# Fewer products in each step of a blocked recurrence, and a quarter of a gate's matrix product on the vector engine

## The chip, the cores and the metric

The kernel runs on one core of one Trainium2 chip. A core has TensorE (PE, the matmuls; PEld in a profile is its weight loads), VectorE (DVE), ScalarE (ACT), GpSimd (POOL), the queue of SyncE (SP) and 16 DMA engines. The metric is the time of one execution in device microseconds; a figure for a kernel is the median of its runs.

## The reference

One layer of a hybrid block over 256 context and 256 latent tokens with 2048 channels: modulation of a normalised input by SiLU(c), one wide input projection, three mixers (neighbourhood attention, pooling, a two-way recurrence), their merge by sigmoid gates, an output projection, and a gated residual. The two parts that the change touches:

```python
# modulation: shift, scale (used at once) and gate (used at the very end)
m = silu(c) @ w_mod + b_mod                   # (2048,) @ (2048, 6144)
shift, scale, gate = split(m, 3)
...
# mixer C, per head: state S is 64 x 64, [value, key]; 16 heads, 2 directions, 512 tokens
def step(S, inp):
    rt, vt, wt, kt, at, bt = inp
    sa = S @ at
    S = S * wt[None, :] + outer(sa, bt) + outer(vt, kt)
    return S, S @ rt
...
out = merged @ w_out
x_out = rms_norm(x + gate * out, final_g)     # latent tokens only
```

## The kernel before

**Numbers.** Matrix products in full precision are made of three products of rounded pairs: each weight tile is split into a high part (`whi`, ScalarE, line 576) and a low part (`wlo`, VectorE, line 577), and activations into `hh` and `hl`. A product of a tile is then hh x whi, hl x whi and hh x wlo.

**Stage one** (about the first 146 us) runs over 16 slices j of the model dimension. Each pass multiplies `cs`, which holds SiLU(c) of latent and context tokens in its columns 1 and 0, with the slice's modulation weights (`adaln_a`: two loads `wm_0` and `wm_1` of 1 MB, 16 matmul records each into `psm`), turns the sums by two transposes, forms shift and scale (`adaln_b`, `md` on VectorE), writes the normalised input `hh[j]` (ScalarE) and `hl[j]` (VectorE) in `htile`, and adds the slice's part of the first seven column tiles (`first_tiles`, `acc`, 21 matmuls of 512 columns on `shi`, `slo`). `psm` is a single buffer: the products of the next slice can start when VectorE has read the sums of this one. The order on TensorE in this stage is set by the framework's scheduler from its own cost estimates, except for instructions marked `keep_in_program_order`.

**Mixers and merge** (to about 1465 us). TensorE's order is written out by a planner, `Order`. It fills TensorE's time with units, halves of 512 KB weight loads: column tiles of the input projection (`d`, line 871), groups of merge logits and then 12 branch groups (`dg`, lines 582 to 584, the branch groups read `bh` and `bl`). Between units it puts bursts of small streams: attention (`side`), the recurrence of one head pair after the other (`rwkv(p)`, p = 0 to 7), folding of the gate (`gate_out`). A stream yields `(TensorE time, latency)` after each burst and comes up again when the latency has passed in planned time; it yields a name to wait for a mark. Weights come into three `raw` buffers over SP's queue in the same order.

**The recurrence** is worked in chunks of 64 tokens, four of context (q = 0) and four of latent tokens (q = 1), for two heads (par) and two directions (d) at once. `features` and `scores` make, for each chunk, EO (operands with the state, rows of value terms), AT (0:4 the strictly triangular matrix A of the chunk, 4:8 the readout's scores), BKT (B and K turned) and SV (state and values above each other). `inverse` inverts I - A: the diagonal 32 x 32 blocks on VectorE over a trip through DRAM (`dA`, `iA`, `dT`, `AT`), and `merge` the block off the diagonal by two small products (`mp`, 64 records each). `chain` then does eight steps, each of three dependent bursts:

```python
px = EO . SV                    # what the state and the values put in      (line 374)
xs = copy(px);  pu = inverse . xs;  SV <- copy(pu)          # lines 376 to 390
pS = BKT . SV;  SV of the next step <- pS * G + sg          # line 398 to 407
```

and for q = 1 also the readout, `py`, from EO and SV (line 382) and from AT and SV (line 411). `sg` is the old state times the decay, four instructions on GpSimd (line 370). `rwkv(p + 1)` is added to the planner when the merge of pair p is done. After the chain comes `readout`; the last pair's result goes through DRAM into `bh[11]`, `bl[11]`, and the four branch groups of this mixer wait for the mark `rw7`.

**The gate.** `gate_units` loads the gate's 16 MB of modulation weights in 64 pieces of 256 KB (`wg`) between units once the attention is done, and multiplies them with `cs` in 32 bursts of 4 matmuls (`mg`, line 1138). For each quarter cc of the columns, the sums are copied to `gs`, the bias row is loaded into one row of `gs`, and a product with `selg` adds them up over partitions and spreads the sum (`pg`, line 1115), which goes to DRAM (`gd[cc]`) for the output stage.

## Time and profile before

| | us |
|---|---|
| median of 3 runs | 1567.87 (1566.26 to 1570.13) |
| profiled execution | 1565.28 |
| its span on the core | 1563.6 |
| stage one, to the last acc matmul | about 146 |
| branch groups | about 1262 to 1466 |

In a row of the timeline stand the start and the length of an instruction or of a run of equal ones, the engine, the line and the tiles as out<-in with the number of records; in brackets the idle time of the engine before it and what ended it. A matmul of 4-byte numbers that is not split leaves two records. Lengths of matmuls overlap, so the distance of two starts tells what one costs. In a row of groups follow the busy time, the mean length in ns and the idle time before. A row of windows has for each engine the busy time and the number of instructions in the order PE, PEld, DVE, ACT, POOL, then the granted clock of TensorE, the DMA share and GB/s.

### The profile page before, as it was taken

The numbers are of one execution on the slowest core, as the hardware profiler recorded it, in microseconds if no ns is written. First come the engines' busy times: TensorE is split into PE (matmuls) and PEld (weight loads), VectorE is DVE, ScalarE is ACT, GpSimd is POOL, SyncE is SP. The second block draws the span as 40 slices with busy tenths as digits, with TensorE's granted clock in tenths as the row PEclk, the third lists the DMA queues.
The fourth block names the chain that finished last, engine by engine and source line by source line (L and its number), as shares of the span: only waits on it lengthen the run. The fifth ranks groups of instructions, "written<-read, shape, count | busy, mean of one in ns | idle before, by whom it ended". The sixth has DMA issues, their size and how long they took to land.

```text
span 1563.6 us, 32275 instructions
## 1 busy us (share of the span) xinstructions
PE 1510.7 (97%) x12256; PEld 1199.3 (77%) x12256; DVE 1133.1 (72%) x2602; ACT 798.5 (51%) x1599; POOL 248.5 (16%) x438
## 2 busy tenths in 40 slices
PE   7999999999999999999999999999999999998998
PEld 5667878798877897788789877877896665667787
DVE  5345788788887877886887768778777775566664
ACT  4224663575465546544664556356646633334453
POOL 2332010150022022201230230023023200210000
PEclk9999999999999999999999999999999999999999
DMA  9996445545532464243355524523566698878863
GB/s 391 348 330 223 144 143 169 163 152 179 173 126 91 137 180 147 95 132 122 100 175 159 179 77 132 175 104 118 167 198 211 202 299 274 268 242 262 267 207 111
DMA packets 217811, 288.21 MB, mean 184 GB/s; under 512 B 62516, under 2 KB 176308, under 8 KB 213048
## 3 DMA queue, kind: packets, MB, share of 16 engines
q1 hardware_dynamic: 210160, 275.66, 54.3%
q10 hardware_dynamic: 7496, 10.50, 1.9%
q8 instruction: 96, 1.57, 0.4%
q14 instruction: 59, 0.48, 0.1%
HBM read 264.34 MB, written 21.50 MB: 183 GB/s over the span
## 4 chain that ended last, share of the span: by engine, by line
PE 86%; DVE 5%; DMA 4%; ACT 2%; issue 2%; SPq 0%; ACTq 0%; POOL 0%; DVEq 0%; POOLq 0%
PE d L871 36%; PE dg L582 9%; PE dg L583 7%; PE dg L584 7%; PE acc L793 2%; PE o L582 2%; DMA raw<-in_w_br 2%; PE o L584 2%; PE o L583 2%; PE px L374 2%; PE acc L799 1%; PE acc L796 1%; PE pu L388 1%; PE pS L398 1%; PE psm L693 1%
## 5 line engine op out<-in xcount | busy, mean ns | idle before, releaser
L576 ACT CAST whi<-raw 128x512 fp32r<-128x512 f32 x584 | 354.0, 619 | 388.7 <-PE d L871 169.5
L577 DVE TENSOR_TENSOR wlo<-raw,whi 128x512 fp32r<-128x512 f32 x584 | 400.4, 698 | 131.3 <-ACT whi L576 100.0
L871 PE MATMUL d<-hh,whi 128*128 128x256 f32 (+1 forms) x1184 | 367.5, 330 | 1.1 <-ACT mth L967 1.1
L871 PE MATMUL d<-hl,whi 128*128 128x256 f32 (+1 forms) x1184 | 359.3, 323 | 0.0
L871 PEld LDWEIGHTS d<-hh,whi 128*128 128x128 f32 x1184 | 225.4, 190 | 24.3 <-issue 2.9
L871 PE MATMUL d<-hh,wlo 128*128 128x256 f32 (+1 forms) x1184 | 241.4, 323 | 0.0
L871 PEld LDWEIGHTS d<-hl,whi 128*128 128x128 f32 x1184 | 225.9, 191 | 16.2 <-issue 0.2
L871 PEld LDWEIGHTS d<-hh,wlo 128*128 128x128 f32 x1184 | 183.0, 191 | 16.9 <-issue 0.7
L370 POOL TENSOR_SCALAR sg<-SV,G 64x64 f32<-64x64 f32 x192 | 111.4, 586 | 355.7 <-DVE SV L407 194.1
L582 PE MATMUL dg<-whi,hh 128*128 128x512 f32 x384 | 164.0, 427 | 0.4 <-DVE gnag L911 0.3
L584 PE MATMUL dg<-wlo,hh 128*128 128x512 f32 x384 | 150.7, 392 | 0.8 <-DVE wlo L577 0.6
L583 PE MATMUL dg<-whi,hl 128*128 128x512 f32 x384 | 150.6, 392 | 0.0
L582 PE MATMUL dg<-whi,bh 128*128 128x512 f32 x192 | 83.3, 434 | 10.4 <-ACT whi L576 3.0
L582 PEld LDWEIGHTS dg<-whi,hh 128*128 128x128 f32 x384 | 72.0, 187 | 23.6 <-issue 5.9
L584 PEld LDWEIGHTS dg<-wlo,hh 128*128 128x128 f32 x384 | 72.1, 188 | 17.9 <-DVE wlo L577 1.6
L583 PEld LDWEIGHTS dg<-whi,hl 128*128 128x128 f32 x384 | 72.4, 188 | 10.0 <-issue 0.2
L584 PE MATMUL dg<-wlo,bh 128*128 128x512 f32 x192 | 77.5, 404 | 0.5 <-DVE wlo L577 0.5
L583 PE MATMUL dg<-whi,bl 128*128 128x512 f32 x192 | 77.3, 403 | 0.5 <-DMA bl<-bs 0.5
L309 DVE TENSOR_TENSOR iM<-iA,iT 128x126 f32<-128x126 f32 (+22 forms) x248 | 63.6, 257 | 17.3 <-DMA iA<-dA 10.7
L311 DVE TENSOR_TENSOR iT<-iT,iM 128x126 f32<-128x126 f32 (+22 forms) x248 | 62.8, 253 | 6.6
L806 ACT ACTIVATE hh<-xT,md 128x256 fp32r<-128x256 f32 x32 | 17.5, 593 | 90.5 <-DVE md L717 90.5
L1283 DVE TENSOR_TENSOR wl<-raw,wh 128x512 fp32r<-128x512 f32 x64 | 41.3, 686 | 25.2 <-ACT wh L1282 25.0
(329 smaller groups left out, 2488.6 us busy)
## 6 DMA issues: line engine op xcount, KB each, us to landing
raw<-in_w_in SPq DMA_DIRECT2D x244, 512.0 KB, 3.6
wm<-in_w_ms SPq DMA_DIRECT2D x32, 1024.0 KB, 7.0
raw<-in_w_br SPq DMA_DIRECT2D x48, 512.0 KB, 5.5
wg<-in_w_mg SPq DMA_DIRECT2D x64, 256.0 KB, 4.2
raw<-in_w_out SPq DMA_DIRECT2D x32, 512.0 KB, 4.5
wst<-in_w_st SPq DMA_DIRECT2D x16, 448.0 KB, 7.9
sl<-in_bias SPq DMA_DIRECT2D x32, 128.0 KB, 3.0
iA<-dA SPq DMA_DIRECT2D x16, 256.0 KB, 5.4
```

Of the source, the lines that this page charges most:

```text
L309: nc.vector.tensor_tensor(m, A[:, st:st + 1, st + 1:32].to_broadcast([128, ni, nt]), T[:, 0:ni, st:st + 1].to_broadcast([128, ni, nt]), AL ...
L311: nc.vector.tensor_tensor(T[:, 0:ni, st + 1:32], T[:, 0:ni, st + 1:32], m, ALU.add)
L370: nc.gpsimd.tensor_scalar(sg[hv[par], d], SV[hv[par], par, w, d], G[hv[par], gs[d][0], d:d + 1], None, ALU.mult)
L374: nc.tensor.matmul(px[hv[par], d], EO[:, par, d, cs[d], :], SV[:, par, w, d], start=True, stop=True, tile_position=(0, 64 * par))
L576: nc.scalar.copy(hi, src)
L577: nc.vector.tensor_tensor(lo, src, hi.bitcast(F32), ALU.subtract)
L582: nc.tensor.matmul(acc, a[0], b[0], start=start, stop=False)
L583: nc.tensor.matmul(acc, a[1], b[0], start=False, stop=False)
L584: nc.tensor.matmul(acc, a[0], b[1], start=False, stop=stop)
L793: mm = nc.tensor.matmul(acc[i], shi[:, c], hh[j], start=(j == 0), stop=False)
L871: nc.tensor.matmul(box[0], w[m >= 8][:, 128 * i:128 * i + 128], x, start=(v == 0 and m == 0), stop=(v == 3 and m == 11))
L1283: nc.vector.tensor_tensor(l, r, h.bitcast(F32), ALU.subtract)
```

## The change

1. `merge` forms the whole 64 x 64 inverse `An` (a second small product gives its other block) and multiplies it into B (`pw`, for both q) once per pair, and into the readout's scores (`pz`, in step 0). A step then has two bursts: SV takes px directly, and `xs` and `pu` are gone.
2. `sg` is made by two instructions on GpSimd in place of four.
3. `rwkv(p + 1)` is added before the merge of pair p; its first features wait for the mark `merge{p}` where they take the merge's buffers.
4. The first quarter of the gate is made in stage one: 8 loads of 512 KB (`g0w`), 16 multiply-adds on VectorE into `g0`, and one product with ones (`gate_first`). `gate_units` keeps three quarters.
5. `gate_out` comes up 6.5 us of planned time after the last `mg` burst in place of 4.0. The subtraction that writes `hl` is kept in program order.

```diff
 def features(...):
         yield 1.0, 2.2
+        if q == 0 and p:
+            yield f"merge{p - 1}"
...
-    def merge(s, p, psp, ptag):
+    def merge(s, p, psp, ptag, psc, ctag):
-        DN = s.fp.tile([128, 16, 32], F32, tag="up", name=f"DN{p}")
-        P = s.fp.tile([128, 16, 32], F32, tag="E", name=f"mP{p}")
+        An = s.fp.tile([128, 16, 64], F32, tag="E", name=f"An{p}")
+        P = s.fp.tile([128, 16, 32], F32, tag="up", name=f"mP{p}")
         for q in range(2):
-            for r1, r2 in rr:
-                nc.vector.transpose(DN[r1, 8 * q:8 * q + 8], at[q][r1, :, 0:32])
+            nc.vector.transpose(An[:, 8 * q:8 * q + 8], at[q])
+        for r1, r2 in rr:
+            nc.gpsimd.memset(An[r1, :, 32:64], 0.0)
...
-                nc.tensor.matmul(ps2[r1, i], P[r2, i], at[i // 8][r2, i % 8, 32:64], start=True, stop=True,
-                                 tile_position=(64 * h + 32, 64 * h))
+                d2 = at[i // 8][r2, i % 8, 32:64]
+                nc.tensor.matmul(ps2[r2, i], d2, P[r2, i], start=True, stop=True, tile_position=(64 * h + 32, 64 * h + 32))
+                nc.tensor.matmul(ps2[r1, i], P[r2, i], d2, start=True, stop=True, tile_position=(64 * h + 32, 64 * h))
+        for h, (r1, r2) in enumerate(rr):
+            (nc.scalar.copy if h else nc.vector.tensor_copy)(An[r2, :, 0:32], ps2[r2])
...
-        yield 0.9, 2.2
+        yield 1.4, 2.4
+        for q in range(2):
+            pw = (psp, psc)[q].tile([128, 2, 4, 64], F32, tag=(ptag, ctag)[q], name=f"pw{p}_{q}")
+            for d in range(2):
+                for c in range(4):
+                    for par in range(2):
+                        nc.tensor.matmul(pw[hv[par], d, c], An[hv[par], 8 * q + 2 * c + d], s.BKT[p, q][hv[par], par, d, c],
+                                         start=True, stop=True)
+            for par in range(2):
+                (nc.scalar.copy if par else nc.vector.tensor_copy)(s.BKT[p, q][hv[par], par], pw[hv[par]])
+        s.An = An
+        yield 1.8, 2.4
 def chain(...):
-                    for d in range(2):
-                        nc.gpsimd.tensor_scalar(sg[hv[par], d], SV[hv[par], par, w, d], G[hv[par], gs[d][0], d:d + 1], None, ALU.mult)
+                    nc.gpsimd.tensor_tensor(sg[hv[par]], SV[hv[par], par, w], g2[hv[par]].unsqueeze(2).to_broadcast([64, 2, 64]), ALU.mult)
...
-            xs = s.fp.tile([128, 2, 64], F32, tag="xs", bufs=2, name=f"xs{p}_{i}")
-            nc.vector.tensor_copy(xs, px)
...
-            yield (0.9 if q else 0.45), (1.0 if q else 1.6)
-            pu = psp.tile([128, 2, 64], F32, tag=ptag, name=f"pu{p}_{i}")
-            for d in range(2):
-                for par in range(2):
-                    nc.tensor.matmul(pu[hv[par], d], AT[hv[par], cs[d], d, :], xs[hv[par], d], start=True, stop=True)
             for par in range(2):
-                (nc.scalar.copy if par else nc.vector.tensor_copy)(SV[hv[par], par, w], pu[hv[par]])
-            yield 0.4, 2.0
+                (nc.scalar.copy if par else nc.vector.tensor_copy)(SV[hv[par], par, w], px[hv[par]])
+            if i == 0:
+                pz = psy.tile([128, 8, 64], F32, tag=ytag, name=f"pz{p}")
+                at = s.AT[p, 1][:, 4:8].rearrange("p c d t -> p (c d) t")
+                for k in range(8):
+                    for par in range(2):
+                        nc.tensor.matmul(pz[hv[par], k], s.An[hv[par], 8 + k], at[hv[par], k], start=True, stop=True)
+                nc.scalar.copy(at, pz)
+            yield (0.9 if q or i == 0 else 0.45), (2.0 if q or i == 0 else 2.3)
 # stage one
-            nc.vector.tensor_tensor(hl[j], hf, hh[j].bitcast(F32), ALU.subtract)
+            tc.keep_in_program_order(nc.vector.tensor_tensor(hl[j], hf, hh[j].bitcast(F32), ALU.subtract))
...
+        g0 = wp.tile([P, 512], F32, tag="mt", bufs=2, name="g0")
+        nc.sync.dma_start(g0, rows[0:1, 0:512].to_broadcast([P, 512]))
+        def gate_load(k):
+            raw = g0w[k] = wp.tile([P, 2, 512], F32, tag="raw", bufs=NRAW, name=f"g0w{k}")
+            nc.sync.dma_start(raw, w_mg[0, k])
+        def gate_add(k):
+            if k == 0:
+                tc.keep_in_program_order(nc.vector.tensor_scalar(g0, g0, 1.0 / P, None, ALU.mult))
+            raw = g0w.pop(k)
+            for i in range(2):
+                tc.keep_in_program_order(nc.vector.scalar_tensor_tensor(g0, raw[:, i], cs[:, 2 * k + i, 1:2], g0, ALU.mult, ALU.add))
...
+                if j % 2 and j > 2:
+                    gate_add(j // 2 - 1)
+                if j % 2 == 0:
+                    gate_load(j // 2)
                 first_tiles(j, (4, 5, 6))
             else:
                 first_tiles(j, range(7))
+                gate_add(6)
+        gate_add(7)
 # mixers
             yield from R.inverse(p)
-            yield from R.merge(p, psm, "m")
             if p < 7:
                 O.add(rwkv(p + 1), 2 + p + 1)
+            yield from R.merge(p, psm, "m", psc, "c")
+            O.mark(f"merge{p}")
...
         def gate_out(cc, gs):
-            yield 0.0, 4.0
+            yield 0.0, 6.5
...
+        def gate_first():
+            on = np_.tile([P, P], F32, tag="vT", name="on")
+            nc.gpsimd.memset(on, 1.0)
+            yield 0.0, 1.5
+            pg = psn.tile([P, 512], F32, tag="o", name="pg0")
+            nc.tensor.matmul(pg, on, g0, start=True, stop=True)
+            nc.scalar.copy(g0, pg)
+            nc.scalar.dma_start(gd[0], g0)
+            yield 1.1, 0.0
...
-            return [... for cc in range(4) for h in range(2) for k in range(8)]
+            return [... for cc in range(1, 4) for h in range(2) for k in range(8)]
```

**What it does to the order.** Three places show how instructions move.

TensorE in stage one, from the transposes of one pass (`psm<-ident,ms`) over its last acc tile to the next pass. Before:

```order
L710 MATMUL psm_907<-ident,ms_930 128x128 x2
L793 MATMUL acc_389<-hh_126,shi_893 128x512
L796 MATMUL acc_389<-hh_126,slo_894 128x512
L799 MATMUL acc_389<-hl_142,shi_893 128x512
L693 MATMUL psm_970<-wm_0_971,cs 32x256 x8
L793 MATMUL acc_386<-hh_127,shi_956 128x512
L796 MATMUL acc_386<-hh_127,slo_957 128x512
L793 MATMUL acc_387<-hh_127,shi_956 128x512
```

Now:

```order
L729 MATMUL psm_924<-ident,ms_947 128x128 x2
L812 MATMUL acc_389<-hh_126,shi_908 128x512
L815 MATMUL acc_389<-hh_126,slo_909 128x512
L818 MATMUL acc_389<-hl_142,shi_908 128x512
L812 MATMUL acc_386<-hh_127,shi_973 128x512
L815 MATMUL acc_386<-hh_127,slo_974 128x512
L812 MATMUL acc_387<-hh_127,shi_973 128x512
L815 MATMUL acc_387<-hh_127,slo_974 128x512
L812 MATMUL acc_388<-hh_127,shi_973 128x512
L712 MATMUL psm_989<-wm_0_990,cs 32x256 x8
L815 MATMUL acc_388<-hh_127,slo_974 128x512
```

The first half of the next slice's modulation product (`wm_0`) has gone behind five matmuls that read the new `hh`. This is so in seven of the 15 passes, every second one; in the very first it has gone behind two.

TensorE at a chain's last step (pair 5), from px on. Before:

```order
L374 MATMUL px_7_13618<-SV_1_11863,EO_1_11860 64x64 x4
L382 MATMUL py_7_13625<-EO_1_11860,SV_1_11863 64x64 x4
L582 MATMUL dg_13211<-whi_13563,hh_127 128x512
L583 MATMUL dg_13211<-whi_13563,hl_143 128x512
L584 MATMUL dg_13211<-wlo_13564,hh_127 128x512
L582 MATMUL dg_13281<-whi_13527,hh_126 128x512
L583 MATMUL dg_13281<-whi_13527,hl_142 128x512
L584 MATMUL dg_13281<-wlo_13528,hh_126 128x512
L388 MATMUL pu_7_13645<-xs_7_13623,AT_1_11861 64x64 x4
L582 MATMUL dg_13281<-whi_13563,hh_127 128x512
L583 MATMUL dg_13281<-whi_13563,hl_143 128x512
L584 MATMUL dg_13281<-wlo_13564,hh_127 128x512
```

Now:

```order
L393 MATMUL px_7_13503<-SV_1_11717,EO_1_11714 64x64 x4
L399 MATMUL py_7_13508<-EO_1_11714,SV_1_11717 64x64 x4
L601 MATMUL dg_13305<-whi_13324,hh_122 128x512
L602 MATMUL dg_13305<-whi_13324,hl_138 128x512
L603 MATMUL dg_13305<-wlo_13325,hh_122 128x512
L601 MATMUL dg_13305<-whi_13455,hh_123 128x512
L602 MATMUL dg_13305<-whi_13455,hl_139 128x512
L603 MATMUL dg_13305<-wlo_13456,hh_123 128x512
L601 MATMUL dg_13385<-whi_13324,hh_122 128x512
L602 MATMUL dg_13385<-whi_13324,hl_138 128x512
L603 MATMUL dg_13385<-wlo_13325,hh_122 128x512
L430 MATMUL py_7_13508<-AT_1_11715,SV_1_11717 64x64 x4
```

The burst `pu` between px and the next use of SV is gone; the use of SV follows px after nine unit matmuls.

SP's queue where the last pair's result is stored (`bs<-grwg`) and loaded again (`bh`, `bl`). Before:

```order
L903 DMA bs_1_3_117<-grwg_13890 128x256
L1271 DMA gate<-gd_78 128x512
L564 DMA raw_17567<-in_w_br 128x4x256
L627 DMA bh_17517<-bs_0_3_113 128x2x256
L627 DMA bl_17519<-bs_1_3_117 128x2x256
L564 DMA raw_17597<-in_w_br 128x4x256
```

Now:

```order
L945 DMA bs_1_3_117<-grwg_15436 128x256
L1179 DMA wg_0_7_17473<-in_w_mg 128x2x256
L583 DMA raw_17488<-in_w_br 128x4x256
L646 DMA bh_17494<-bs_0_3_113 128x2x256
L646 DMA bl_17496<-bs_1_3_117 128x2x256
L583 DMA raw_17531<-in_w_br 128x4x256
```

The store stood ahead of the last 11 of the 48 loads of branch weights (`raw<-in_w_br`) and now stands ahead of the last 18. Of the gate's loads `wg`, 38 of 64 came after the first load of branch weights, now 43 of 48.

More of the change, by code (lines that the diff above doesn't have):

```diff
@@ L323, in inverse @@
         yield 0.0, 10.5
-    def merge(s, p, psp, ptag):
+    def merge(s, p, psp, ptag, psc, ctag):
         nc = s.nc
+        hv = (slice(0, 64), slice(64, 128))
         at = [s.AT[p, q][:, 0:4].rearrange("p c d t -> p (c d) t") for q in range(2)]
-        DN = s.fp.tile([128, 16, 32], F32, tag="up", name=f"DN{p}")
-        P = s.fp.tile([128, 16, 32], F32, tag="E", name=f"mP{p}")
+        An = s.fp.tile([128, 16, 64], F32, tag="E", name=f"An{p}")
+        P = s.fp.tile([128, 16, 32], F32, tag="up", name=f"mP{p}")
         ps1 = psp.tile([128, 16, 32], F32, tag=ptag, name=f"mp1{p}")
@@ L338, in merge @@
             for h, (r1, r2) in enumerate(rr):
-                nc.tensor.matmul(ps1[r2, i], at[i // 8][r1, i % 8, 32:64], DN[r1, i], start=True, stop=True,
+                nc.tensor.matmul(ps1[r2, i], at[i // 8][r1, i % 8, 32:64], An[r1, i, 0:32], start=True, stop=True,
                                  tile_position=(64 * h, 64 * h + 32))
@@ L364, in chain @@
             cs = (w, 3 - w)
-            gs = ((i, 0), (i + 1, 1))
             if 0 < i < 7:
                 sg = s.fp.tile([128, 2, 64], F32, tag="sg", bufs=2, name=f"sg{p}_{i}")
+                g2 = G.rearrange("p a b -> p (a b)")[:, 2 * i:2 * i + 4:3]
                 for par in range(2):
-                    for d in range(2):
-                        nc.gpsimd.tensor_scalar(sg[hv[par], d], SV[hv[par], par, w, d], G[hv[par], gs[d][0], d:d + 1], None, ALU.mult)
+                    nc.gpsimd.tensor_tensor(sg[hv[par]], SV[hv[par], par, w], g2[hv[par]].unsqueeze(2).to_broadcast([64, 2, 64]), ALU.mult)
             px = psp.tile([128, 2, 64], F32, tag=ptag, name=f"px{p}_{i}")
@@ L401, in chain @@
                     for d in range(2):
-                        g = G[hv[par], gs[d][0], d:d + 1]
+                        g = G[hv[par], i + d, d:d + 1]
                         o = SV2[hv[par], par, j % 4, d]
@@ L813, in htile @@
             held[j] = (shi, slo)
+        g0 = wp.tile([P, 512], F32, tag="mt", bufs=2, name="g0")
+        nc.sync.dma_start(g0, rows[0:1, 0:512].to_broadcast([P, 512]))
+        g0w = {}
+        def gate_load(k):
[7 more added lines that the diff above has]
+                tc.keep_in_program_order(nc.vector.scalar_tensor_tensor(g0, raw[:, i], cs[:, 2 * k + i, 1:2], g0, ALU.mult, ALU.add))
         htile(0)
@@ L1147, in load @@
                 return [mult]
-            return [lambda cc=cc, h=h, k=k: load(cc, h, k) for cc in range(4) for h in range(2) for k in range(8)]
+            return [lambda cc=cc, h=h, k=k: load(cc, h, k) for cc in range(1, 4) for h in range(2) for k in range(8)]
         todo = []
@@ L1219, in hybrid_block @@
         loads = [8, 9, 10, 11]
+        O.add(gate_first(), 0)
         O.add(side(), 0)
```

## The prediction

> **What bounds the kernel now.** I read the page first, then TensorE's waits, then the stages by window, then single stretches of TensorE's timeline.
>
> ```profile
> span 1563.6 us, 32275 instructions
> PE 1510.7 (97%) x12256; PEld 1199.3 (77%) x12256; DVE 1133.1 (72%) x2602; ACT 798.5 (51%) x1599; POOL 248.5 (16%) x438
> PE 86%; DVE 5%; DMA 4%; ACT 2%; issue 2%; SPq 0%; ACTq 0%; POOL 0%; DVEq 0%; POOLq 0%
> ```
>
> TensorE (PE) is busy 97% of the span and is 86% of the chain that ended last. So an instruction taken from another engine is worth nothing unless TensorE stood waiting for it, and every matmul added or removed counts at what TensorE needs for it. The waits (engine and line, what it waited for, us in total, times, longest) tell what else there is:
>
> ```profile
> PE dg L582 <- ACT whi L576: 3.0, 2, 1.6
> PE pS L398 <- ACT SV L390: 3.0, 2, 1.8
> PE dg L582 <- DMA bh<-bs: 2.9, 1, 2.9
> PE pg L1115 <- DMA gs<-in_rows: 2.7, 1, 2.7
> PE acc L793 <- ACT hh L806: 1.7, 1, 1.7
> ```
>
> No wait is large; the change touches the last four. The stages, with the granted clock in the third column from the right and then the DMA share and rate:
>
> ```profile
> 40.00:80.00 40.00, 39.12 (x294) 24.47 (x292) 16.29 (x45) 10.83 (x18) 12.13 (x5) 1.00 0.94 343
> 480.00:500.00 20.00, 18.20 (x138) 13.75 (x138) 14.95 (x33) 11.31 (x27) 7.28 (x14) 0.91 0.15 53
> 1260.00:1280.00 20.00, 17.54 (x76) 12.96 (x74) 12.23 (x34) 8.90 (x14) 0.00 (x0) 0.91 0.94 279
> 1300.00:1320.00 20.00, 17.02 (x88) 10.21 (x88) 7.92 (x15) 5.15 (x11) 0.00 (x0) 0.91 0.89 260
> 1340.00:1360.00 20.00, 17.34 (x114) 11.07 (x114) 11.40 (x25) 6.47 (x12) 4.01 (x8) 0.95 0.90 285
> 1360.00:1380.00 20.00, 20.00 (x167) 13.40 (x165) 10.43 (x26) 6.72 (x15) 5.23 (x12) 0.97 0.76 238
> 1420.00:1440.00 20.00, 17.54 (x73) 14.17 (x74) 11.93 (x21) 8.00 (x15) 0.00 (x0) 0.91 0.84 277
> ```
>
> Stage one (the first row) has TensorE and the DMA engines both near full. Elsewhere each longer wait costs twice: the clock falls to 0.91 of a 20 us window, 1.8 us of full-speed time, right where the waits are. I take 1.7 for each such fall (0.05 + 0.03 of two windows, 1.6 us, after the wait of pg).
>
> [...]
>
> **The recurrence on TensorE.** A burst costs its own length and some 0.1 us at either edge, read between start times of neighbouring matmuls (start, length):
>
> ```profile
> 488.61 0.39 PE L871 MATMUL d<-hh,whi 128*128 128x512 f32 x1
> 488.93 0.45 PE L388 MATMUL pu<-xs,AT 64*64 64x64 f32 x8
> 489.30 0.50 PE L871 MATMUL d<-hl,whi 128*128 128x512 f32 x1
> 489.64 0.40 PE L871 MATMUL d<-hh,whi 128*128 128x512 f32 x1
> 479.87 0.45 PE L388 MATMUL pu<-xs,AT 64*64 64x64 f32 x8
> 480.25 0.73 PE L125 MATMUL psw<-lt,wa 128*128 128x256 f32 x4
> 364.48 0.68 PE L230 MATMUL pv<-ident,mxv 64*64 64x64 f32 x16
> 365.10 0.50 PE L582 MATMUL dg<-whi,hh 128*128 128x512 f32 x1
> 1164.60 1.20 PE L339 MATMUL mp<-DN,AT 32*32 32x32 f32 x64
> 1165.73 0.38 PE L871 MATMUL d<-hh,whi 128*128 128x256 f32 x1
> 483.14 0.45 PE L411 MATMUL py<-AT,SV 64*64 64x64 f32 x8
> 483.52 0.97 PE L871 MATMUL d<-hh,wlo 128*128 128x512 f32 x3
> 1186.14 0.64 PE L1138 MATMUL mg<-wg,cs 128*32 128x256 f32 x8
> 1186.71 0.50 PE L582 MATMUL dg<-whi,hh 128*128 128x512 f32 x1
> ```
>
> ```profile
> L388 PE MATMUL pu<-xs,AT 64*64 64x64 f32 x512 | 28.7, 230 | 0.0
> L347 PE MATMUL mp<-AT,mP 32*32 32x32 f32 x512 | 9.6, 192 | 0.4 <-ACT mP L342 0.4
> L1138 PE MATMUL mg<-wg,cs 128*32 128x256 f32 x256 | 20.9, 399 | 0.0
> L986 DVE SCALAR_TENSOR_TENSOR bth<-bth,dg 128x512 f32<-128x512 f32 x16 | 10.9, 682 | 7.5 <-PE dg L584 7.5
> ```
>
> A d matmul of 512 columns takes 0.23, so a pu burst that stands alone costs 489.64 - 488.61 - 0.46 = 0.57, and one that another burst follows 0.38 (480.25 - 479.87). The rows count 512 records, 8 to a burst: 64 bursts, 24.3 to 36.5 us. I take 0.50, for most stand alone: **-32**.
>
> Added for each of the 8 head pairs: the pw products, 32 matmuls or 64 records. 16 records (pv) cost 0.62 + 0.20 at the edges = 0.82, so 8 more cost about 0.24, and a burst of 64 costs 0.57 + 7 x 0.24 = 2.25. Eight: **+18.0** (by the 28.7 of the pu row for as many records, up to 28.7; by the 1.13 per 64 of the mp row, 9.0). The pz products are 32 records behind px: 0.38 (the row of py, 483.14 to 483.52) + 3 x 0.24 = 1.10, eight times **+8.8** (4.5 to 14.4 by the same two rows). The second product of merge doubles the 64 records of mp: 1.13 each (1164.60 to 1165.73), **+9.0**; no row has two such products on the same rows of the array, so 7.9 (without edges) to 18.
>
> The quarter of the gate removes 8 of the 32 mg bursts, 0.38 joined to 0.77 alone (0.57 + 0.20): 3.0 to 6.2, taken **-5.0**. The fold pg of that quarter stays, as one matmul on ones. Bursts in sum: -32 + 18.0 + 8.8 + 9.0 - 5.0 = **-1.2**.
>
> What VectorE and ScalarE lose (xs, 64 copies) and gain (copies of An, BKT and pz) is about even and lies under TensorE's 97%; without that cover it would be a microsecond at each of 8 merges. POOL's fewer sg instructions free an engine that is 16% busy: nothing. The wait for px by SV and of pS for SV is the one that pu and pS had, so the 3.0 us row of pS stays. The features that wait for the mark of merge hold back only VectorE work of the next pair, which is now queued a merge sooner.
>
> **Stage one.** The order moves psm for the next tile behind five acc matmuls in every second pass, and these need hh:
>
> ```profile
> 86.09 0.40 PE L799 MATMUL acc<-hl,shi 128*128 128x512 f32 x1
> 86.42 1.07 PE L693 MATMUL psm<-wm,cs 128*32 128x256 f32 x16
> 86.50 1.09 ACT L806 ACTIVATE hh<-xT,md 128x256 fp32r<-128x256 f32 x2 [5.78 <-DVE md L717]
> 87.64 0.50 PE L793 MATMUL acc<-hh,shi 128*128 128x512 f32 x1
> 139.94 0.69 DVE L577 TENSOR_TENSOR wlo<-raw,whi 128x512 fp32r<-128x512 f32 x1
> 142.14 0.50 PE L793 MATMUL acc<-hh,shi 128*128 128x512 f32 x1 [1.72 <-ACT hh L806]
> 123.66 1.69 SPq L564 DMA_DIRECT2D raw<-in_w_in  x3
> ```
>
> Today psm fills the time in which ScalarE writes hh (86.50 to 87.59). With psm behind, TensorE stands still from 86.32 to 87.64, and psm's 1.0 us comes on top later. Seven full places and the first pass: 8 x 1.0 = **+8.0** (7.2 to 9.8). The hole is 1.2 us; the 1.72 before 142.14 left the clock whole, so I charge no clock.
>
> That 1.72 is a subtraction of column weights (139.94) put between two steps of md. The new order has none there: **-1.6**. In exchange four gate additions of 0.68 stand ahead of the first column weights on VectorE, and the second and third weight loads, issued at 123.66 now, wait for the buffers of gate loads until the end of the stage: between 0 and 4 us, taken **+1.6** (two of the 0.68). The other additions fall into VectorE's idle time (16 of 40 us busy). On SP's queue a gate load of 512 KB follows every second wm pair; it takes the buffer of the gate load three before it, which VectorE adds up in pass 2k + 3, a pass and a half before SP comes to load k + 3. Two passes then move 5.64 MB, 16.4 us at 343 GB/s, as long as two passes with a hole (15.4 + 1.0); at 343 / 0.94 it is 15.4. So the DMA costs nothing more.
>
> **Late stage.** The fold pg is recorded 2.5 us later, so its wait of 2.7 and the clock fall behind it go: -2.5 - 1.7 = **-4.2** (0 to -4.4). The last pair's result is now stored with 18 loads of branch weights still behind it on SP's queue, 11 before, about 20 us of TensorE's work: the wait of 2.9 for bh, 0.5 for bl and a clock fall go, **-5.1** (0 to -5.1). Between 1260 and 1320 the branch weights land late (two falls to 0.91, 3.0 us of whi waits). The inverse's scattered copies come sooner and 5 gate loads more come in the branch stage, 43 for 38, though few at its start: between -6 and +4.5, taken **-2.0**.
>
> Sum: -1.2 + 8.0 - 1.6 + 1.6 - 4.2 - 5.1 - 2.0 = **-4.5 us**. The profiled execution took 1565.28, 2.6 less than the median of the runs shown, 1567.87; from the median the forecast is 1563.4, or 1563.
>
> **Rivals.** (1) The bursts are cheaper: if all pu bursts stood alone, 4.5 more go, and if the waits of pS (3.0, with the clock fall of 1.7 in the row of 480) go with the shorter steps, 4.7: 1554. For it: 97% busy, and a third fewer bursts; against: the copy that pS waited for is still there. (2) The holes of stage one trip the clock: a fall costs 1.7, and if two thirds of 8 do, +9.1: 1572.5. For it: the waits of 1.8 (pS, the row of 480) and 1.6 (whi, the row of 1300) come with falls; against: 1.72 did not. (3) The last pair does not finish sooner, since features and inverse set its pace: 5.1 lost, 1568.5. Against: one dependent copy of three goes from each step. (4) Slower: the late stage goes at the pace of its transfers. For it: shares of 0.94 and 0.89 with TensorE waiting. Then the 4.2, 5.1 and 2.0 come back as waits for weights, and 5 more gate loads (1.31 MB at 279 GB/s) cost 4.7: +11.5, 1579.4. It decides once 9.2 of these are lost. Against: 0.76 at 1360 with TensorE never idle. (5) The clock falls late in the kernel stay, set off by the shorter waits around, and only the waits go: 3.4 lost, 1566.8. Against: between the falls the clock row is back near 1.00. [...]
>
> **How the numbers follow.** Forecast 0.42, with its own range of 1557 to 1569; rival 1 0.24, rival 2 0.08, rival 3 0.07, rival 4 0.16, rival 5 0.03. A measurement of this kernel tells 0.3% (4.7 us) from no change. The forecast lies at that edge: 0.22 of it below 1563.2, 0.20 within. Faster 0.22 + 0.24 = 0.46; same 0.20 + 0.08 + 0.07 + 0.03 = 0.38; slower 0.16. The range 1551 to 1574 takes in rivals 1, 2, 3 and 5 and leaves out rival 4 and little else.
>
> **What would show it.** Right: no pu rows, pw in eight bursts near 2.2 us, waits of acc for hh of some 8 us in stage one, no wait of pg for gs and none of dg for the last bh. Wrong: clock falls before 146 us, more than 5 us of new waits between 146 and 1180, or more waits for branch weights after 1240.

## The result, and the profile after

The changed kernel takes 1604.6 us (1600.2 to 1605.7, median of 4 runs), the kernel before beside it 1567.1: a ratio of 1.0235, with a 95% interval of 1.0206 to 1.0263. It is 37.6 us slower, where 1563 was forecast. The profiled execution took 1600.2, the fastest of the four. From its page:

```profile
span 1598.5 us, 33599 instructions
PE 1508.4 (94%) x12960; PEld 1211.6 (76%) x12960; DVE 1167.3 (73%) x2563; ACT 817.7 (51%) x1634; POOL 190.6 (12%) x359
PE 43%; DVE 7%; DMA 4%; ACT 3%; issue 2%; SPq 0%; POOL 0%; ACTq 0%; DVEq 0%; POOLq 0%
```

TensorE is busy for 1508.4 us, 2.3 less than before, in a span that is 34.9 longer. So the time did not go into matmuls: TensorE stands. The waits that matter below, after the change (engine and line, what it waited for, us in total, times, longest):

```profile
PE pw L366 <- issue: 15.9, 7, 5.8
PE acc L812 <- ACT hh L825: 11.8, 11, 1.8
PE dg L603 <- DVE wlo L596: 5.9, 6, 2.1
PE dg L601 <- ACT whi L595: 5.8, 4, 2.0
PE py L430 <- ACT SV L402: 3.9, 5, 1.2
PE pm L109 <- DVE ym L103: 3.4, 3, 1.3
PE mg L1191 <- DMA wg<-in_w_mg: 2.7, 1, 2.7
PE pw L366 <- ACT AT L359: 1.8, 1, 1.8
```

The largest such row before was 3.0 us in total, apart from the first load. Now the new product pw waits in all eight pairs, 17.8 us together, and stage one's acc matmuls wait 11.8 for hh, where some 8 were forecast. The stages (stage one from its first to its last acc matmul, the main stage up to the first branch group, the branch groups; the first branch group before the change starts at 1271.6, not at 1262), first before; behind the length stand the busy time of PE, PEld, DVE, ACT and POOL, the granted clock, the DMA share and GB/s:

```profile
25.30:147.30 122.00, 118.24 (x836) 76.27 (x833) 50.24 (x136) 33.79 (x54) 39.27 (x36) 0.99 0.86 317
147.30:1271.60 1124.30, 1107.07 (x9711) 909.83 (x9710) 885.39 (x2056) 630.97 (x1297) 190.96 (x363) 1.00 0.48 152
1271.60:1465.80 194.20, 180.68 (x1154) 126.82 (x1155) 123.30 (x271) 74.36 (x141) 13.36 (x24) 0.96 0.84 269
```

and after:

```profile
24.78:157.97 133.19, 122.56 (x848) 76.72 (x849) 70.61 (x149) 32.62 (x51) 39.33 (x37) 0.98 0.84 317
157.97:1312.84 1154.87, 1104.93 (x10296) 923.02 (x10294) 908.12 (x2046) 649.82 (x1331) 140.47 (x293) 0.99 0.46 144
1312.84:1500.36 187.52, 177.93 (x1275) 126.17 (x1275) 114.59 (x228) 75.69 (x144) 5.80 (x14) 0.98 0.90 286
```

Stage one is 11.2 us longer, the main stage 30.6, the branch groups 6.7 shorter; the rest (the start 0.5 shorter, the output stage 0.4 longer) cancels. In the main stage PE's busy time fell by 2.1, so its 30.6 are waits. How one wait of pw comes about is seen on VectorE, ScalarE and TensorE in the second pair:

```profile
457.60 0.69 DVE L596 TENSOR_TENSOR wlo<-raw,whi 128x512 fp32r<-128x512 f32 x1
458.30 0.68 DVE L356 COPY An<-mp 32x512 f32<-32x512 f32 x1
459.02 0.58 ACT L356 COPY An<-mp 32x512 f32<-32x512 f32 x1 [1.79 <-DVE An L356]
459.63 0.41 DVE L359 COPY AT<-mp 32x256 f32<-32x256 f32 x1 [0.65 <-ACT An L356]
460.07 0.36 ACT L359 COPY AT<-mp 32x256 f32<-32x256 f32 x1 [0.48 <-DVE AT L359]
460.47 0.41 DVE L359 COPY AT<-mp 32x256 f32<-32x256 f32 x1 [0.43 <-ACT AT L359]
460.91 0.36 ACT L359 COPY AT<-mp 32x256 f32<-32x256 f32 x1 [0.48 <-DVE AT L359]
455.23 0.39 PE L603 MATMUL dg<-wlo,hh 128*128 128x512 f32 x1
461.38 3.68 PE L366 MATMUL pw<-BKT,An 64*64 64x64 f32 x64 [5.76 <-issue]
```

The first seven rows are VectorE and ScalarE, the last two TensorE. The second merge product ended at 452.6. Its result leaves by six copies, and each starts when the one on the other engine has ended: VectorE, ScalarE, VectorE and so on, 3.0 us from 458.30 to 461.27. The first of them stood behind column weights (wlo) and features on VectorE. TensorE had three or four microseconds of other work planned and stood from 455.6 to 461.4. The plan in `merge` (`yield 1.4, 2.4`) has pw come 2.4 us after the product; in the trace it was 4.1 to 8.8 us. The profile names a releaser for one of the eight waits only ("issue" means that it shows none), but in all eight pairs pw starts 0.1 us after the last copy of AT has ended.

### The profile page after: what moved, and what is told of

It is laid out like the page before. It is cut to its first block, busy times and chain, and to the rows that moved or that the text cites. A ratio compares the mean times of both kernels' runs of the same rounds, so it can differ in the third digit from the quotient of the medians.

```text
span 1598.5 us, 33599 instructions
## 1 busy us (share of the span) xinstructions
PE 1508.4 (94%) x12960; PEld 1211.6 (76%) x12960; DVE 1167.3 (73%) x2563; ACT 817.7 (51%) x1634; POOL 190.6 (12%) x359
## 4 chain that ended last, share of the span: by engine, by line
PE 43%; DVE 7%; DMA 4%; ACT 3%; issue 2%; SPq 0%; POOL 0%; ACTq 0%; DVEq 0%; POOLq 0%
PE d L913 17%; PE dg L601 5%; PE dg L603 4%; PE dg L602 4%; DVE wlo L596 2%; PE o L603 2%; PE o L601 2%; PE o L602 2%; DMA raw<-in_w_br 1%; PE px L393 1%; PE pS L417 1%; ACT whi L595 1%; PE pw L366 1%; PE mg L1191 1%; DMA wg<-in_w_mg 1%
## 5 line engine op out<-in xcount | busy, mean ns | idle before, releaser
L913 PE MATMUL d<-hh,wlo 128*128 128x256 f32 (+1 forms) x1184 | 236.6, 321 | 2.2 <-DVE wlo L596 2.1
L603 PEld LDWEIGHTS dg<-wlo,hh 128*128 128x128 f32 x384 | 73.1, 190 | 26.2 <-DVE wlo L596 9.8
L601 PE MATMUL dg<-whi,bh 128*128 128x512 f32 x192 | 82.2, 428 | 7.7 <-ACT whi L595 4.3
L389 POOL TENSOR_TENSOR sg<-SV,G 64x128 f32<-64x128 f32 x96 | 49.0, 510 | 190.3 <-DVE SV L424 152.4
L812 PE MATMUL acc<-hh,shi 128*128 128x512 f32 x112 | 49.7, 443 | 12.5 <-ACT hh L825 11.8
```

The source lines that it names most:

```text
L389: nc.gpsimd.tensor_tensor(sg[hv[par]], SV[hv[par], par, w], g2[hv[par]].unsqueeze(2).to_broadcast([64, 2, 64]), ALU.mult)
L601: nc.tensor.matmul(acc, a[0], b[0], start=start, stop=False)
L603: nc.tensor.matmul(acc, a[0], b[1], start=False, stop=stop)
L812: mm = nc.tensor.matmul(acc[i], shi[:, c], hh[j], start=(j == 0), stop=False)
L913: nc.tensor.matmul(box[0], w[m >= 8][:, 128 * i:128 * i + 128], x, start=(v == 0 and m == 0), stop=(v == 3 and m == 11))
```

## The experiments

Every kernel of the study in one table. Idle is the idle time ahead of TensorE's matmuls, summed over the trace; half is half of the time that the clock stood at half speed, which is the most that it can have cost; rest is the span less both, roughly TensorE's work at full speed. Kernels with the same matmuls (after, e1, e3, e4, e6 to e8, c4, f1 to f4) differ by up to 6.7 us in this column, so it is good to some 3 us. "Main" is the idle time between the last acc matmul and the first branch group, "pw" the part of pw. Times are medians, ratios are against the kernel before on the same chip.

| kernel | us | ratio (95%) | idle | half | rest | main | pw |
|---|---|---|---|---|---|---|---|
| before | 1567.1 | 1 | 45.1 | 14.0 | 1504.4 | 14.8 | |
| after | 1604.6 | 1.0235 (1.0206 to 1.0263) | 82.2 | 19.7 | 1496.6 | 48.3 | 17.8 |
| e1_due: 6.5 us ahead of pw | 1585.3 | 1.0108 (1.0063 to 1.0154) | 69.1 | 26.2 | 1491.8 | 30.4 | 0 |
| e7_split: pw in two, other buffer | 1589.0 | 1.0128 (1.0099 to 1.0157) | 73.8 | 17.3 | 1496.6 | 31.2 | 1.0 |
| e6_prio: merge's copies first | 1604.8 | 1.0221 (1.0200 to 1.0242) | 81.5 | 23.7 | 1498.5 | 46.4 | 15.7 |
| e2_nog: no gate in stage one | 1605.3 | 1.0241 (1.0202 to 1.0280) | 77.0 | 26.8 | 1500.6 | 47.9 | 17.2 |
| e3_actq: gate loads by ScalarE | 1606.7 | 1.0254 (1.0212 to 1.0296) | 85.8 | 25.0 | 1493.8 | 50.4 | 17.7 |
| e4_late: features as before | 1608.1 | 1.0255 (1.0205 to 1.0304) | 89.3 | 25.8 | 1493.0 | 44.5 | 7.1 |
| e5_due_nog: e1 and e2 | 1594.2 | 1.0148 (1.0120 to 1.0176) | 62.2 | 33.2 | 1495.8 | 28.6 | 0.7 |
| e8_lat: longer plan, copies first | 1600.9 | 1.0193 (1.0167 to 1.0219) | 79.5 | 26.5 | 1495.2 | 36.6 | 0 |
| c4_step7: longer plan elsewhere | 1595.1 | 1.0161 (1.0133 to 1.0190) | 73.7 | 27.1 | 1492.8 | 31.6 | 1.0 |
| f1_act: e7, gate loads by ScalarE | 1588.3 | 1.0119 (1.0097 to 1.0140) | 68.7 | 26.8 | 1492.5 | 31.9 | 1.0 |
| f2_due5: 5.0 us ahead of pw | 1587.4 | 1.0115 (1.0092 to 1.0137) | 68.4 | 20.4 | 1496.3 | 28.8 | 2.5 |
| f3_due8: 8.0 us ahead of pw | 1592.0 | 1.0136 (1.0109 to 1.0162) | 67.4 | 30.5 | 1494.4 | 24.1 | 0 |
| f4_split36: e7, other plan | 1595.6 | 1.0161 (1.0135 to 1.0187) | 70.0 | 28.7 | 1498.1 | 28.1 | 0.1 |
| c1_ctrl: before, 0.8 us in merge | 1585.7 | 1.0102 (1.0071 to 1.0133) | 57.7 | 18.2 | 1503.4 | 23.8 | |
| c2_ctrl: before, 0.6 us in features | 1580.6 | 1.0083 (1.0050 to 1.0115) | 58.5 | 16.8 | 1503.8 | 21.2 | |
| c3_gate: before, gate in stage one | 1581.3 | 1.0073 (1.0051 to 1.0095) | 60.3 | 24.7 | 1497.2 | 20.6 | |

Between before and after: idle +37.1, half clock +5.7, TensorE's work -7.8; together the 35.0 of the span. The change did save TensorE work, and gave it back about five times over in standing.

### The wait of pw

**e1_due** gives the copies their time in the plan.

```diff
-        yield 1.4, 2.4
+        yield 1.4, 6.5
```

> The changed kernel with one number altered: the planner brings pw up 6.5 us after the merge's second product instead of 2.4. Theory (the six copies out of the merge's second product run one after the other on VectorE and ScalarE, 4.1 to 8.8 us from that product to pw, and pw shares its one PSUM buffer; the plan allows 2.4): the eight waits of pw, 17.8 us, fall below 4, two or three clock falls go with them, 1583 to 1588 us. Rival (VectorE is simply too full around the merge, the wait moves to px, py or wlo as the recurrence starts 4 us later): pw's waits go, as much comes back elsewhere, 1598 to 1606.

1585.3 us, and no row of pw is left among the waits; those that lead now, apart from the first load:

```profile
PE acc L812 <- ACT hh L825: 11.9, 12, 1.8
PE dg L601 <- DMA bh<-bs: 7.1, 1, 7.1
PE dg L601 <- ACT whi L595: 4.8, 1, 4.8
PE mp L353 <- ACT mP L347: 4.3, 2, 2.7
```

One number in the planner is worth 19 us, about what pw waited (17.8), and the main stage's idle time fell by as much (48.3 to 30.4). The theory holds, except for the clock falls: its trace, of the slowest of its four executions, has more half clock (26.2 against 19.7). And the kernel is still 18 us behind the one before, with a new wait of 7.1 for bh, the last pair's result.

**e6_prio** leaves the 2.4 and raises the priority of the merge's copies to that of the chain's (300), to lift them ahead of the column weights in the engines' queues.

```diff
+            yield 300
             yield from R.merge(p, psm, "m", psc, "c")
```

> The changed kernel, with the merge's copies in the same raised priority as the chain's, so that they stand ahead of column weights on VectorE and ScalarE; pw stays planned 2.4 us after the second product. Theory (the six copies alone take 3.0 us and pw waits for the last of them): the long waits shrink, but each stays at 1 us or more, 8 to 12 us for all eight against 17.8, 1592 to 1600. Rival (the queue ahead of the copies is all of it): pw's waits below 5, 1583 to 1589; or the column weights behind them come late instead, 1600 to 1606.

pw still waited 15.7 us, more than either said, and the time did not move. pw came 4.1 to 6.6 us after the product here, against 4.1 to 8.8 in the change: the longest came down. But the raised priority did not clear the copies' way: in the third pair a scan of the next pair's features (`up`, 1.24 us on VectorE, at 602.87) still stands between the copies of An and those of AT. So this run does not tell the copies from the queue around them; e4_late, below, does.

**e7_split** tells which of the six pw needs. In the change the first pw goes into the merge's PSUM buffer, a single one that the second product still fills; here it goes into the recurrence's, in a burst of its own.

```diff
-        yield 1.4, 2.4
+        yield 1.4, 3.2
         for q in range(2):
-            pw = (psp, psc)[q].tile(..., tag=(ptag, ctag)[q], ...)
+            pw = (psc, psp)[q].tile(..., tag=(ctag, ptag)[q], ...)
...
-        s.An = An
-        yield 1.8, 2.4
+            s.An = An
+            yield 1.0, 2.4 if q == 0 else 2.4
```

> The changed kernel with pw in two bursts: the first (context) into the recurrence's own PSUM buffer and 3.2 us of planned time after the second product, the other one 2.4 us later into the merge's. Theory (the first pw needs the two copies of An only, and stood behind the four copies of AT because its buffer was the merge's): waits of the first below 0.7 us each, of the second below 0.7 too, 1583 to 1590. Rival (pw waits for AT's copies in any case, since one counter per engine tells it of all copies): 6 to 12 us of waits stay, 1592 to 1600.

1589.0; one wait of 1.0 us is left. In the fourth pair (TensorE, then ScalarE):

```profile
756.79 1.15 PE L366 MATMUL pw<-BKT,An 64*64 64x64 f32 x32
754.78 0.58 ACT L356 COPY An<-mp 32x512 f32<-32x512 f32 x1
757.61 0.36 ACT L359 COPY AT<-mp 32x256 f32<-32x256 f32 x1
758.51 0.36 ACT L359 COPY AT<-mp 32x256 f32<-32x256 f32 x1 [0.54 <-DVE AT L359]
```

pw starts 1.4 us after the copies of An, while those of AT are still to come. In seven of the eight pairs it starts 0.8 to 3.3 us before the last copy of AT has ended, in the first as it ends. So the four copies of AT had stood in its way through the shared buffer alone. The rival's one counter per engine is in the trace after (all 1363 instructions of ScalarE that signal raise one semaphore, all 2201 of VectorE another), yet here pw did not wait for the last copy of AT.

### Stage one

The hole as it looks after the change (TensorE, then ScalarE):

```profile
67.05 0.38 PE L729 MATMUL psm<-ident,ms 128*128 128x128 f32 x2
67.73 0.40 PE L818 MATMUL acc<-hl,shi 128*128 128x512 f32 x1
69.28 0.50 PE L812 MATMUL acc<-hh,shi 128*128 128x512 f32 x1 [1.15 <-ACT hh L825]
68.13 1.09 ACT L825 ACTIVATE hh<-xT,md 128x256 fp32r<-128x256 f32 x2 [5.80 <-DVE md L736]
```

**e2_nog** takes the quarter out of stage one.

```diff
-        g0, g0w, gate_load, gate_add, gate_first, and their calls
-            ... for cc in range(1, 4) ...
+            ... for cc in range(4) ...
```

> The changed kernel with the gate's first quarter back among the other three (no loads, multiply-adds or fold of it in stage one). Theory: the last acc matmul ends near 147 us instead of 158, with no waits of acc for hh but the old one of 1.7; the quarter costs eight mg bursts, about 4 us, later; 1595 to 1598. Rival (the holes come from the kept order of hl and not from the gate): stage one as long as before this edit, 1604 to 1609.

The last acc matmul ends at 148.1, as the theory has it, but nothing is won: 1605.3, within the rival's range without its cause. The work of TensorE rises by 4.0 us (eight mg bursts), and the half clock by 7.1.

**e3_actq** keeps the quarter and restores the order of psm, by issuing the loads from another queue; that the framework's estimate for SyncE's queue had put psm late is a guess.

```diff
-            nc.sync.dma_start(raw, w_mg[0, k])
+            nc.scalar.dma_start(raw, w_mg[0, k])
```

> The changed kernel with the gate's eight stage-one loads issued from ScalarE's queue instead of SyncE's; TensorE's order then has psm of the next slice ahead of the acc matmuls in all passes again, and all loads and multiply-adds stay. Theory (the 1.15 us holes are psm's place alone): the holes go, a pass takes 7.7 us, 10 to 12 us less, 1592 to 1595. Rival (the DMA engines, 338 to 382 GB/s at a share of 0.92 to 0.98 in stage one, set 16.6 us for two passes): waits of psm for wm take the holes' place, 1600 to 1605.

The holes go, a pass takes 7.7 us again, and the DMA engines carry what that needs:

```profile
40.00:56.00 16.00, 15.70 (x118) 9.77 (x119) 6.10 (x16) 3.85 (x6) 4.92 (x2) 1.00 1.02 417
```

417 GB/s: the rival, a stage paced by transfers, is out. But the stage ends only 3.3 us sooner, and the whole took 1606.7, slower than either side said. Three loads came at the very start and held up wm there (2.9 us), and at the end the weights of the first column tile came so late that their subtraction stood in the middle of md (VectorE, then TensorE):

```profile
145.75 0.69 DVE L596 TENSOR_TENSOR wlo<-raw,whi 128x512 fp32r<-128x512 f32 x1 [2.79 <-ACT whi L595]
146.36 0.22 DVE L735 TENSOR_SCALAR md<-md,pp 128x2 f32<-128x2 f32 x1
147.95 0.50 PE L812 MATMUL acc<-hh,shi 128*128 128x512 f32 x1 [4.50 <-ACT hh L825]
```

**f1_act** holds each of these loads in its place behind hh, on top of e7_split.

```diff
-            nc.sync.dma_start(raw, w_mg[0, k])
+            tc.keep_in_program_order(nc.scalar.dma_start(raw, w_mg[0, k]))
...
+                if e == 0:
+                    tc.keep_in_program_order(<the activation that writes hh>)
```

> pw in two bursts as above (1589.0), and the gate's stage-one loads on ScalarE's queue, each kept in its place behind the slice's hh, so that psm is ahead of the acc matmuls again in all passes but the first and no load comes early. Theory (the holes of stage one are a loss of their own, 7 x 1.15 us, and the column weights at the stage's end come 1 to 3 us later): stage one ends 5 to 8 us sooner and the whole is 1581 to 1585. Rival (what stage one gains is lost again, as with the loads on ScalarE's queue before, where the weights after the stage came late): 1587 to 1592.

Stage one ends 3.9 us sooner than in e7_split, less than expected, for the wait at its end is still 4.4; then column weights are waited for, 3.9 more, and the whole takes the same time (1588.3 against 1589.0). The rival holds: the gate's loads use the three weight buffers (three column weight loads go out only at 146.4, one ahead of them at 139.9), so what stage one gains is waited for behind it.

**c3_gate** has the quarter alone, on the kernel before.

```diff
+        g0, g0w, gate_load, gate_add, gate_first, and their calls, as in the change
-            yield 0.0, 4.0        # gate_out
+            yield 0.0, 6.5
```

> The kernel before, with the first quarter of the gate in stage one (loads, multiply-adds, fold, kept order of hl) and the fold's 6.5 us; old recurrence, features as before. Theory (stage one's eight holes and its first pass cost 10 to 11 us, eight mg bursts less and the waits of pg gain 6 to 12 in the late stage): 1564 to 1574. Rival (the quarter is a plain loss): 1575 to 1580.

1581.3 (1.0073), just above the rival's range: here the quarter of the gate is a loss. TensorE's work fell by 7.2 us, stage one grew by 11.6, and the main stage had 5.8 more of waits.

### The other small waits

With pw's waits gone or nearly so, the main stage still idles 24 to 37 us against 14.8. Three kernels went for single causes.

**e4_late** puts the features of the next pair back behind the merge.

```diff
-            if p < 7:
-                O.add(rwkv(p + 1), 2 + p + 1)
             yield from R.merge(p, psm, "m", psc, "c")
             O.mark(f"merge{p}")
+            if p < 7:
+                O.add(rwkv(p + 1), 2 + p + 1)
```

> The changed kernel with rwkv(p + 1) added after the merge of pair p, as before the change; all else stays. Theory (the next pair's features, now beside the chain, put reciprocals and table loads ahead of the chain's copies: waits of py 3.9, pm 3.4, mp 2.0 and wlo 8 us): 8 to 12 us of these go, 1592 to 1597; pw's waits stay near 17. Rival (these waits come from where the planner happens to put things, or from the shorter chain itself): as many elsewhere, and the last pair ends later, 1600 to 1610.

1608.1. The waits of py, pm and pw shrank, and others took their place: pt for SV 4.9, bh 6.9. In time the rival holds. But pw's wait fell from 17.8 to 7.1, which the theory had left near 17: pw came 3.9 to 4.6 us after the product instead of 4.1 to 8.8. In the change, in the sixth pair, the scan of the next pair's features (1.40 us on VectorE, at 1043.70) stands between the copies of An and of AT; here it does not. By this run some 7 us of pw's wait are the copies, with column weights between them, against a plan that is too short, and some 11 are work that the earlier features (item 3 of the change) put among them.

**e8_lat** and **c4_step7** write longer times into the plan where e1 still waited.

```diff
 e8_lat:   -  yield 0.9, 2.4   (ahead of the second product)      +  yield 0.9, 4.4
           -  yield 1.4, 2.4                                      +  yield 1.4, 6.0
           +  yield 300 ahead of merge
 c4_step7: -  yield 0.9, 2.4                                      +  yield 0.9, 3.2
           -  yield 1.4, 2.4                                      +  yield 1.4, 6.5
           -  2.0 behind px of the last step                      +  3.5
```

> Planned times as the copies really take them: 4.4 us ahead of the merge's second product instead of 2.4, 6.0 ahead of pw instead of 2.4, and the merge's copies in raised priority. Theory (the plan's times were short, and TensorE stood at each): waits of pw and of the second product for mP and An, 8.6 us with 6.5 alone, fall below 3; with their clock falls 1575 to 1582. Rival (the last pair's result is late already, a wait of 7.1 us for bh with 6.5 alone, and comes later still): 1584 to 1592.

> The changed kernel with 6.5 us ahead of pw, 3.2 instead of 2.4 ahead of the merge's second product and 3.5 instead of 2.0 behind px of the last step, where py waited for SV. Theory (each of these waits goes, 2.5 us of py and 4.3 of mP with 6.5 alone): 1576 to 1582. Rival (waits of the same size appear at other places of the new order): 1584 to 1592.

Both are slower than e1 (1600.9 and 1595.1), beyond what either side expected. In e8_lat the waits moved to the column weights that now stood behind the copies (wlo 8.8 us in the main stage, 2.0 in e1); in c4_step7 to wlo (6.0) and gnag (7.6, 3.2 in e1). Mending the plan wait by wait did not converge in these two.

So the question was put to the kernel before: **c1_ctrl** and **c2_ctrl** each alter one planned latency of it and nothing else.

```diff
 c1_ctrl:  -  yield 0.9, 2.2   (behind the second merge product)  +  yield 0.9, 3.0
 c2_ctrl:  -  yield 1.0, 2.2   (first burst of the features)      +  yield 1.0, 2.8
```

> The kernel before, with one planned latency altered: 3.0 instead of 2.2 us behind the merge's second product, which costs the recurrence 0.8 us per pair by itself and shifts all that the planner puts behind it. Theory A (the order before fits the engines' real times by being tuned, and any new order has some 15 us more of small waits in the main stage, as every variant of the change had): idle TensorE time between the last acc matmul and the first branch group grows from 15 to 22 or more, 1575 to 1590 us. Theory B (the small waits belong to the new recurrence): it stays near 15 and the time at 1565 to 1572.

> The kernel before, with 2.8 instead of 2.2 us behind the first burst of the features (16 places). As for the other altered latency: Theory A 22 us or more of waits in the main stage, 1575 to 1590; Theory B near 15, 1565 to 1572.

They lose 1.0% and 0.8%, 16 and 11 us by the medians, with the same work (rest 1503.4 and 1503.8 against 1504.4). The largest waits of the main stage in c1_ctrl:

```profile
PE S L1057 <- DVE gnag L1086: 5.0, 3, 2.7
PE pk L259 <- DVE EO L277: 3.1, 2, 2.2
PE pb L259 <- ACT BKT L244: 2.8, 1, 2.8
```

and in c2_ctrl:

```profile
PE S L1057 <- DVE gnag L1086: 2.9, 2, 1.6
PE px L374 <- DVE SV L405: 2.8, 3, 1.7
PE pb L259 <- ACT BKT L244: 2.8, 1, 2.8
```

They are waits for the same engines as after the change, and none is large; both kernels also waited for bh (6.1 and 7.0 us, 2.9 before). Theory A holds in time, and for idle time in one of the two (23.8, and 21.2 where 22 was said). Two orders shifted by less than a microsecond lost 11 and 16 us; that the order before fits the engines' real times unusually well is the reading that agrees with this. Both edits lengthen a planned latency, so part of the loss (3.2 and 4.1 us, by the wait for bh) can be a recurrence that simply ends later. No run alters the order without lengthening anything.

**e5_due_nog, f2_due5, f3_due8, f4_split36** ask whether the new recurrence adds to that.

```diff
 e5_due_nog: e1_due and e2_nog together
 f2_due5:   -  yield 1.4, 2.4    +  yield 1.4, 5.0
 f3_due8:   -  yield 1.4, 2.4    +  yield 1.4, 8.0
 f4_split36: e7_split with 3.6 and 3.0 for 3.2 and 2.4
```

> The 6.5 us of planned time ahead of pw, and the gate's first quarter not in stage one but with the other three: what is left is the new recurrence and the earlier features. Theory (pw's wait is most of the loss of the recurrence, and the quarter of the gate is worth nothing either way, since stage one loses some 10 us by it and the late stage gains as much): as fast as with 6.5 alone, 1581 to 1588. Rival (the holes of stage one are a loss of their own that only the chance order of the late stage hid): 1574 to 1579.

> The changed kernel with 5.0 us ahead of pw, instead of 2.4 or 6.5. Theory (pw's waits are gone from some 5 us on, and beyond them it is chance how a new order fits the other engines): pw's waits below 5, idle time in the main stage 24 to 36, the whole anywhere from 1578 to 1598. Rival (small waits are a cost of the new recurrence that a planned latency does not alter): within 3 us of the kernel with 6.5, 1582 to 1588, and idle time of 30 to 32.

> The changed kernel with 8.0 us ahead of pw. As with 5.0: by the theory 1578 to 1598 with idle time of 24 to 36 in the main stage, by the rival 1582 to 1588 with 30 to 32; a later recurrence adds up to 3 us of waits for bh at the end in either case.

> pw in two bursts with 3.6 and 3.0 us ahead of them, instead of 3.2 and 2.4. Both already had no wait worth naming, so whatever moves is the order of all that stands behind: by the theory of chance 1578 to 1602, by the rival 1586 to 1592.

e5_due_nog was slower than both its theories said, though its interval overlaps that of e1. The other three took 1587.4, 1592.0 and 1595.6 with 28.8, 24.1 and 28.1 of idle time: the spread is larger than the rival allows, so chance of the order has a part. It may not be all. Three variants of the kernel before (c1 to c3) stand at 1.0073 to 1.0102, eight of the new recurrence with at most 2.5 us of pw's waits and without raised priority (e1, e5, e7, c4, f1 to f4) at 1.0108 to 1.0161, though TensorE has less work in them. The intervals of the two groups overlap. Whether this last half per cent is chance again or the denser work of VectorE and ScalarE around the shorter steps stays open. No version found beats the kernel before.

## Why the prediction was wrong

**The step that failed** is in the paragraph on the recurrence: what VectorE and ScalarE lose and gain by copies "lies under TensorE's 97%; without that cover it would be a microsecond at each of 8 merges". The copies of An, BKT and pz were costed at nothing, with a reserve of 8 us that went into no end of the range. The trace shows 2.2 us at each merge (17.8), and e1 that removing it gives 19. The prediction counted copies as work on engines with time to spare. They are a chain: six in a row after a product, through one PSUM buffer, against a planned 2.4 us that stands in the diff. The next sentences failed with it: the earlier features were to "hold back only VectorE work of the next pair", and e4 shows that their work on VectorE among the copies made some 11 of the 17.8.

**A term was missing.** The sum takes every stage of before with its small waits and adds and removes pieces. But the planner lays out the whole main stage anew after an edit, and in c1_ctrl and c2_ctrl an edit of one latency cost 11 and 16 us with the matmuls unchanged. That the same happened in the change is argued, not shown: with pw's waits taken out by e1, the main stage still idles 30.4 us against 14.8. pw's waits, these small waits and stage one make up the loss.

**Bursts on TensorE**, forecast -1.2 with the gate: TensorE's work fell by 7.8, good to some 3. The mis-sized term is merge's second product, taken at +9.0 (7.9 to 18). TensorE in the second pair, from the first record of the doubled product to the next matmul:

```profile
451.29 0.21 PE L353 MATMUL mp<-mP,AT 32*32 32x32 f32 x1
452.51 0.38 PE L913 MATMUL d<-hh,whi 128*128 128x256 f32 x1
```

1.22 us for 128 records, where 64 took 1.13: the added half cost 0.09 each, 0.7 for eight. The two kinds of records alternate, with starts 8.6 ns apart in the mean, where those of the 64 before lie 16.0 apart. The other two terms were right: a pw burst between units costs 2.21 us in e1 (2.25 said), a pz burst 1.08 (1.10 said).

**Stage one**, forecast +8.0 - 1.6 + 1.6: +11.2 measured. The seven holes were right in place and size (1.15 us each; such a pass takes 8.9 us instead of 7.7). The first pass took 2.5 us more, where 1.0 was said: a wait of 1.85, and the clock at half for 6.83 us instead of 3.41. The wait of 1.7 at the stage's end did not go (1.57 after). That the transfers cost nothing more was right (no wait for wm in stage one's passes).

**Late stage**, forecast -11.3: -6.7 for the branch groups. The waits of pg for gs and of dg for the last bh went, as said. A wait of mg for wg came (2.7), and whi 1.3 more. The gain at bh was partly luck: in e1, where TensorE no longer stands at pw, bh is waited for 7.1 us again. It seems that the result came in time because TensorE was late itself.

**The rivals.** The slower one, a late stage paced by transfers, named the right sign at the wrong place. The clock in stage one stood at half for one window of 3.41 us more than before, all in the first pass; the holes of 1.15 set off none. Of the three signs given for "wrong", more than 5 us of new waits between 146 and 1180 us is the one that showed clearly, with some 30.

## What to carry to other kernels

Where an order is planned ahead, a change to a dependent chain is costed at the planned latency against the real one: count the copies that follow a product one by one, with what stands ahead of them and between them in the queue and which buffer holds up the next product, before counting matmuls. Ask what the plan's order is worth by itself: shift one latency in the old kernel, and if that costs 1%, no edit that saves less can be read from the sum of its parts. A saving on the busiest engine is only as good as the waits that the new order leaves.

## What the runs showed of the hardware

**The clock.** In the traces before and after, all 15 changes of the granted clock in each lie on one grid of 3.413 us, and each stretch at half lasts one or two steps of it (3.41 or 6.83 us), but for the one that the end of the trace cuts off. Around the wait above, the clock is the third figure from the right (here the first window is idle throughout):

```profile
456.58:459.99 3.41, 0.00 (x0) 0.00 (x0) 2.75 (x6) 1.23 (x3) 0.00 (x0) 1.00 0.48 154
459.99:466.82 6.83, 5.45 (x69) 4.96 (x70) 1.82 (x4) 1.89 (x4) 0.00 (x0) 0.50 0.01 2
466.82:470.23 3.41, 3.41 (x50) 2.86 (x50) 1.58 (x3) 1.44 (x3) 0.00 (x0) 1.00 0.03 7
```

Over the 18 profiles of this study, cut along the grid, windows at full speed in which TensorE idled for 1.85 us or more were followed by one at half 114 times in 116; between 1.55 and 1.85 us 36 in 87; between 1.0 and 1.55 us 13 in 235; below 1.0 us never, in 7571. In the traces before and after alone these are 8 in 8, 8 in 16, 0 in 31 and 0 in 846: each of their 16 falls follows a window with 1.57 to 3.41 us of idle time, and the most idle time without a fall is 1.84 us, in the window from 606.77 after the change. A window of 3.413 us at half is 1.7 us less of full-speed time. The prediction charged this for the waits that stood beside falls and could not say which others would have one.

**VectorE beside GpSimd.** Six of the sixteen gate multiply-adds on VectorE took 2.50 us instead of 0.75 (nanoseconds least, median, most in the first row; then GpSimd and VectorE at one of them, two multiply-adds in the row):

```profile
L849 DVE SCALAR_TENSOR_TENSOR g<-g0w,cs,g x16: 744/752/2502, 62.6 to 155.8; 128x512 f32<-128x512 f32 x16
62.41 2.14 POOL L831 TENSOR_TENSOR slo<-wst,shi 128x896 fp32r<-128x896 f32 x1 [6.53 <-ACT shi L830]
62.60 3.29 DVE L849 SCALAR_TENSOR_TENSOR g<-g0w,cs,g 128x512 f32<-128x512 f32 x2
```

All six began while GpSimd formed slo, and ended half a microsecond after it; five others that began just before slo took the usual 0.75. The prediction had them at 0.68. What held them is not shown. Here it cost TensorE nothing: in all six passes VectorE began to read psm 0.1 us after its last matmul.
